# Rows that every partition needs: through a DRAM scratch and a read with partition step zero, in place of products with a selector

## The chip, the cores and the metric

One core of a Trainium2 chip runs the whole kernel. Times are device microseconds. The kernel before took 2334.57 us, the median of three runs (2333.76 to 2335.11).

## The reference, cut to what matters

Two layers of a backbone work on 256 context tokens and 256 latent tokens, 1024 features each, all in float32. Each layer is a half feed-forward step, three token mixers side by side (windowed attention, gated linear attention, mLSTM), and a second half feed-forward step. The last layer's output is wanted for the latent tokens only. The change is in the mLSTM, which has 4 heads of 128 and runs in both directions:

```python
def mlstm_scan(q, k, v, i_pre, log_f, carry):
    def step(carry, inp):
        C, n, m = carry
        b = jnp.cumsum(fc, axis=-1)
        log_w = jnp.where(tri, b[..., :, None] - b[..., None, :] + ic[..., None, :], -jnp.inf)
        log_inter = b + m[..., None]
        m_i = jnp.maximum(log_inter, jnp.max(log_w, axis=-1))
        w = jnp.exp(log_w - m_i[..., None])
        w_inter = jnp.exp(log_inter - m_i)
        s = jnp.einsum('bhid,bhjd->bhij', qc, kc) * w
        num = (w_inter[..., None] * jnp.einsum('bhid,bhde->bhie', qc, C)
               + jnp.einsum('bhij,bhje->bhie', s, vc))
        den = w_inter * jnp.einsum('bhid,bhd->bhi', qc, n) + jnp.sum(s, axis=-1)
        h = num / jnp.maximum(jnp.abs(den), jnp.exp(-m_i))[..., None]
        ...
```

For each direction and head there are numbers with one value per token: the gate sum in `log_w`, the factor `1 / max(|den|, exp(-m))` and that factor times `w_inter`. Each of them is multiplied or added to a matrix in which the token is the column, so it must be there on all 128 partitions.

## The kernel before, in words

Features lie on the 128 partitions and the 512 tokens (T) on the columns. Layer 0 works on all 512 columns; in layer 1 the query side of each mixer covers only the 256 latent columns (`cs = slice(c0, T)` with c0 = 256). A dense product splits float32 into two float32r parts and takes three matmuls (`acc<-xh,hi`, `acc<-xl,hi`, `acc<-xh,lo`) into an accumulator in PSUM of the pool `acc` (4 buffers); products of the mixers go into the PSUM pool `mx` (4 buffers). Weights come by SyncE's queue into `raw`; ACT writes the high part (L231) and DVE the low part (L232). Nearly every matmul has the line of the helper `mm`, L150; DVE's two-input operations have that of `tt`, L122, and ACT's functions that of `act`, L125.

The mLSTM runs per layer as one call of `mlstm_rows` and two calls of `mlstm`, one for each pair of heads. `mlstm_rows` makes the rows of all four heads and both directions in one tile: row 32 * q + hp belongs to direction and head parity q = 0 to 3 and to pair hp. A call of `mlstm` then builds states (L869) and weights within chunks, for which it needs the gate row `aa` on all partitions (`ab`, used in L883); sums the weights over the partitions with matmuls against `onec` or `onec2` ("the row sums"); makes den and its reciprocal (L905, L907) as rows; and needs both results on all partitions again (`rb`, `wb`) ahead of six matmuls for each of its two heads ("the outputs"), which the norm of the head follows (`head_norm`, with a column sum against `ones_h`, and L480, L481, L630 on DVE).

`bcast` (L833) makes such a tile: two matmuls into a `mx` buffer, whose stationary operand is one column of `sel`, repeated 128 times, so that the product picks row r; one for the high and one for the low part of the rows. The parts are made by `split`: a cast on ACT (L313) and a subtraction on DVE (L314).

The order on each engine is fixed ahead of the run by a scheduler of the tile framework: it takes the program's order as priority and moves work ahead when what it needs is there by its own estimates. So dense products of the mixer's later projections and output branches stand between the small matmuls of the mixers. The pools bound this: `W()` tiles (`t`) are 17, `F()` tiles (`f`) 25. POOL's queue holds, apart from additions for a norm (L493), only the reads that bring the residual back from a scratch in DRAM (`x<-xd`, L1130, 8 per layer).

After the mLSTM comes the attention (QK^T products into `mx` of 128x512, masks, L989 the maximum over keys, L990, exponentials, L999 the scaling, L1006 transposes, L1009 and L1011 copies, L1017), in layer 1 in four blocks.

Of the kernel before, what the change touches and what calls it, by code (L numbers as in the profile page):

```python
# [9 lines left out]
F32 = mybir.dt.float32  # L10
# [10 lines left out]
T = L + S  # L21
# [11 lines left out]
# columns of w_in, in the order the kernel consumes them (gate block first)  # L33
# [15 lines left out]
# columns of the small per-layer parameters  # L49
# [8 lines left out]
# shape-only float tables  # L58
# [19 lines left out]
def hybrid_backbone_kernel(ctx: ExitStack, tc: tile.TileContext, xT, cc, small, tables, lmask, crow, modw, modt,  # L78
# [42 lines left out]
    def tt(o, a, b, op):  # L121
        V.tensor_tensor(o, a, b, op)  # L122

    def act(o, i, f, **k):
        return A.activation(o, i, f, **k)  # L125
# [9 lines left out]
    def load(o, i):  # L135
        """a load; those of the start in the order of the program, and some later ones behind them."""
        d = nc.sync.dma_start(o, i)
        if loads and late[0] < 24:
            order(d, loads[-1])
        if starting[0]:  # L140
            loads.append(d)
        else:
            late[0] += 1

    def exp_ln_tables(after):
        """load the table set that serves both Exp and Ln, behind the activation `after`."""
        order(A.preload_act_table_set("natural_log_exp_and_others"), after, "table set of the next functions")  # L147

    def mm(o, l, r, start=True, stop=True):
        PE.matmul(o, l, r, start=start, stop=stop)  # L150

# [1 line left out]
    ct = res.tile([128, N_CT], F32, name="ct")  # L153
    sel = res.tile([128, 8], F32R, name="sel")
# [42 lines left out]
    def load_tables():  # L197
# [5 lines left out]
        V.tensor_copy(sel[:], C("selm"))  # L203

# [36 lines left out]
    def wunit_f(src, n, raw=None):  # L241
        """the same in tiles of the feature pool, for units that are wanted ahead of their turn."""
# [12 lines left out]
    def ahead(srcs):  # L255
        """the first two units of the next phase."""
# [12 lines left out]
    def dense_with(w, xs, cs):  # L269
        """one tile of 128 output features over the columns cs; K = 128 * len(xs)."""  # L270
# [8 lines left out]
    def dense_halves(ws, xs, done):  # L279
        """some tiles, one stream after the other: starts before the second stream is there."""  # L280
# [9 lines left out]
    def dense_tokens(src, xs):  # L290
        """512 output features with the tokens on partitions: one tile per chunk."""
# [33 lines left out]
    def start(src):  # L325
        """the first norm, the modulation it needs and the first products, as the weights come in."""
# [29 lines left out]
        def features(k):  # L356
            """modulation of the features 128 * k .., then these features of the norm."""
            with tc.high_priority() if k == 0 else ExitStack():
# [9 lines left out]
                for j in range(2):  # L368
                    mm(pt[:, 2 * j:2 * j + 2], sb[:, 128 * j:128 * j + 128], C("sel2"))
# [25 lines left out]
    def load_cond():  # L395
        """silu of the two conditioning vectors, on every partition."""
# [7 lines left out]
    def mod_vec(l, j, cond):  # L404
        """generator: modulation vector j of layer l on the vector engine, 128 features a step."""
# [46 lines left out]
    def mod_scale(l, j):  # L452
        """-0.5 * gain * (1 + scale) of norm j."""
# [7 lines left out]
    def mod_gate(l, j):  # L461
        """half of the gate of sub-layer j."""
# [10 lines left out]
    def neg2rstd(ms, cs, eps_col, eps):  # L473
        """-2 / sqrt(ms + eps): table value with one Newton step."""
# [11 lines left out]
    def square(k, c):  # L486
        """squares of one tile of the stream c, summed over the tiles but the last two."""
# [14 lines left out]
    def adaln(l, j, c0=0):  # L502
        """norm j of layer l: one call of the result for each stream, behind its last residual."""
# [50 lines left out]
    def turn(late, h, gate, nxt):  # L554
        """the last output tiles of a phase by streams, with the norm of the next phase behind each."""
# [11 lines left out]
    def ffn(l, j, c0, fill, pre, xn, side, nxt, head=None):  # L567
        """one half step; pre: the first weights, nxt: where those of the next phase are."""
# [44 lines left out]
    def log_sigmoid(z, bias, out_t, tmp):  # L613
        """log sigmoid(z + bias) = min(z + bias, 0) - ln(1 + exp(-|z + bias|))."""
# [6 lines left out]
    def head_norm(out, o, cs, gcol, eps_col, eps, tabled=True):  # L621
        """-2 * rmsnorm over the partitions of o (PSUM), times gcol."""
# [5 lines left out]
        mm(ms[:, cs], ones_h[:], sq[:, cs])  # L628
# [6 lines left out]
    def gla(l, ft, c0, gq, gk, gv, gb, gw2, gcol):  # L635
# [6 lines left out]
        for d in range(2):  # L642
            z = mx()
            mm(z[:], gw2[:, (2 * d + ft) * 128:(2 * d + ft + 1) * 128], gb[:])
# [13 lines left out]
        # states between chunks  # L658
# [3 lines left out]
        for d in range(2):  # L662
# [17 lines left out]
            for i, c in enumerate(ch):  # L680
                ps = mx()
                for hh in range(2):
                    mm(ps[64 * hh:64 * hh + 64, 0:128], kd[:, i * 128 + 64 * hh:i * 128 + 64 * hh + 64],
                       gv[c][:, hd(2 * ft + hh)])
# [7 lines left out]
        # within chunks  # L692
        att = []
        for hh in range(2):
            ps = mx()
            r = slice(64 * hh, 64 * hh + 64)
            for c in range(q0, 4):
                cc_ = slice(c * 128, (c + 1) * 128)
                mm(ps[:, cc_], gk[r, cc_], gq[r, cc_])
# [3 lines left out]
        for li, s in enumerate(LEVELS):  # L703
# [16 lines left out]
            for hh in range(2):  # L720
                ps = mx()
                r = slice(64 * hh, 64 * hh + 64)
                for c in range(q0, 4):
                    cc_ = slice(c * 128, (c + 1) * 128)
                    mm(ps[:, cc_], ek[r, cc_], eq[r, cc_])
# [4 lines left out]
        # outputs  # L730
# [28 lines left out]
    def conv_silu(l, ps, i, c0):  # L759
        """twice silu(conv(x) + b) of one tile of channels."""  # L760
# [18 lines left out]
    def mlstm_rows(l, gb):  # L779
        selgb = C("selgb")  # L780
        pi, pf = mx(), mx()
        mm(pi[:], selgb[:, 0:128], gb[:])
        mm(pf[:], selgb[:, 128:256], gb[:])
# [22 lines left out]
        # columns r = (head parity within direction q, head pair): index 2 * q + hp  # L806
# [18 lines left out]
        mm(ps[:, 0:64], ones_1[:], dd[:].rearrange("p a b -> p (a b)"))  # L825
# [511 lines left out]
```

## Time and profile before

| what | value |
|---|---|
| runs | 2333.76, 2334.57, 2335.11 us |
| profiled execution, span from first to last instruction | 2333.1 us |
| PE / DVE / ACT / POOL busy in it | 2291.4 / 1533.6 / 975.1 / 53.2 us |
| mean granted clock of TensorE | 0.996 of full speed |
| DMA, mean over the span | 135 GB/s |

The page gives the profiled execution no other time than its span, so the span stands for it below; it is 1.5 us under the median of the runs. PE is busy in nearly every slice of the span. Busy time of PE counts overlapping matmuls, so a mean duration of a group is longer than the spacing of its matmuls in a run.

### The profile page before, as it was taken

Reading aid. Unit: us, or ns where it says so; the run is one execution under the profiler, and the core shown is the slowest. Engines: PE = TensorE matmul, PEld = TensorE weight load, DVE = VectorE, ACT = ScalarE, POOL = GpSimd, SP = SyncE. Lnnn points to the kernel's source line nnn. Section 1 sums busy time; section 2 is a strip of 40 time slices with the busy share of each in tenths; the row PEclk is TensorE's granted clock in tenths of the full one; section 3 lists DMA queues with packets and bytes.
Section 4 is the critical chain, followed back from the end, with each engine's and each line's share of the span. In section 5 each row is a group of like instructions: output and inputs, shape, how many; then the busy total and the mean of one; then the engine's idle time right before and its main releaser. Section 6 shows DMA issues by size and latency. Waiting matters only on the chain. (4 is left out here: it accounts for less than half of the span.)

```text
span 2333.1 us, 32827 instructions
## 1 busy us (share of the span) xinstructions
PE 2291.4 (98%) x12496; PEld 1910.3 (82%) x12496; DVE 1533.6 (66%) x3213; ACT 975.1 (42%) x1569; POOL 53.2 (2%) x65
## 2 busy tenths in 40 slices
PE   7999999999999999999999999999999999999999
PEld 4888888777877667888888898888888788889999
DVE  4686875579865664658833357855545897877755
ACT  4322224445644542342222253222245665745443
POOL 0000001000000000100000000000010000001000
PEclk9999999999999999999999999999999999999999
DMA  7665554212211212436533236655433233335764
GB/s 282 210 200 159 187 187 129 91 48 66 82 55 64 64 46 81 147 111 198 173 113 99 76 115 208 202 160 188 157 114 103 88 100 100 109 120 183 241 199 145
DMA packets 117390, 314.94 MB, mean 135 GB/s; under 512 B 13296, under 2 KB 16240, under 8 KB 117104
## 3 DMA queue, kind: packets, MB, share of 16 engines
q1 hardware_dynamic: 116208, 309.69, 41.3%
q0 software_dynamic: 1024, 3.15, 0.4%
q8 instruction: 98, 1.61, 0.3%
q14 instruction: 60, 0.49, 0.1%
HBM read 308.59 MB, written 4.19 MB: 134 GB/s over the span
## 5 line engine op out<-in xcount | busy, mean ns | idle before, releaser
L231 ACT CAST hi<-raw 128x1024 fp32r<-128x1024 f32 (+2 forms) x446 | 434.6, 977 | 962.7 <-PE acc L150 637.4
L150 PE MATMUL acc<-xh,hi 128*128 128x512 f32 (+1 forms) x2192 | 784.5, 358 | 9.6 <-ACT xh L125 6.3
L150 PE MATMUL acc<-xl,hi 128*128 128x512 f32 (+1 forms) x2192 | 783.9, 358 | 0.2
L150 PE MATMUL acc<-xh,lo 128*128 128x512 f32 (+1 forms) x2192 | 781.7, 357 | 1.6 <-DVE lo L232 1.6
L232 DVE TENSOR_TENSOR lo<-raw,hi 128x1024 fp32r<-128x1024 f32 (+2 forms) x446 | 503.4, 1131 | 322.9 <-ACT hi L231 307.7
L150 PEld LDWEIGHTS acc<-xh,hi 128*128 128x128 f32 x2192 | 415.7, 190 | 76.8 <-ACT xh L125 8.7
L150 PEld LDWEIGHTS acc<-xl,hi 128*128 128x128 f32 x2192 | 415.7, 190 | 66.1 <-issue 8.8
L150 PEld LDWEIGHTS acc<-xh,lo 128*128 128x128 f32 x2192 | 415.7, 190 | 64.4 <-issue 6.7
L150 PE MATMUL acc<-f,hi 128*128 128x512 f32 (+1 forms) x1016 | 352.2, 347 | 0.0
L150 PE MATMUL acc<-f,lo 128*128 128x512 f32 (+1 forms) x896 | 314.1, 351 | 0.0
L415 DVE SCALAR_TENSOR_TENSOR u<-f,f 128x512 f32<-128x512 f32 x448 | 284.6, 685 | 12.7 <-DMA f<-in_modt_dram 12.7
L150 PE MATMUL acc<-t,hi 128*128 128x512 f32 (+1 forms) x824 | 287.1, 349 | 0.0
L150 PEld LDWEIGHTS acc<-f,hi 128*128 128x128 f32 x1016 | 192.2, 189 | 25.0 <-issue 1.2
L150 PEld LDWEIGHTS acc<-f,lo 128*128 128x128 f32 x896 | 169.7, 189 | 22.1 <-issue 0.4
L150 PEld LDWEIGHTS acc<-t,hi 128*128 128x128 f32 x824 | 155.8, 189 | 20.3
L122 DVE TENSOR_TENSOR t<-t,acc 128x512 f32<-128x512 f32 (+1 forms) x90 | 54.9, 610 | 154.8 <-PE acc L150 153.7
L539 DVE SCALAR_TENSOR_TENSOR x<-acc,ggt,x 128x256 f32<-128x256 f32 x136 | 61.1, 479 | 88.5 <-PE acc L150 88.4
L125 ACT ACTIVATE t<-t 128x512 f32<-128x512 f32 (+2 forms) x180 | 93.0, 529 | 58.3 <-DVE t L122 35.7
L122 DVE TENSOR_TENSOR t<-t,f 128x512 fp32r<-128x512 f32 (+3 forms) x172 | 99.2, 585 | 2.9 <-ACT f L313 2.1
L150 PE MATMUL mx<-t,t 64*128 64x128 f32 (+2 forms) x592 | 77.9, 288 | 0.9 <-DVE t L861 0.5
L150 PEld LDWEIGHTS mx<-t,t 64*128 64x128 f32 (+1 forms) x592 | 64.2, 188 | 16.3 <-issue 9.1
L150 PE MATMUL mx<-t,f 128*64 128x256 f32 (+3 forms) x352 | 69.8, 412 | 0.4
(209 smaller groups left out, 2167.3 us busy)
## 6 DMA issues: line engine op xcount, KB each, us to landing
raw<-in_w_dram SPq DMA_DIRECT2D x179, 512.0 KB, 3.6
f<-in_modt_dram SPq DMA_DIRECT2D x256, 256.0 KB, 4.5
raw<-in_win_dram SPq DMA_DIRECT2D x118, 512.0 KB, 3.5
raw<-in_w_dram SPq DMA_DIRECT2D x61, 384.0 KB, 3.1
raw<-in_w_dram SPq DMA_DIRECT2D x61, 320.0 KB, 3.0
raw<-in_wout_dram SPq DMA_DIRECT2D x24, 512.0 KB, 3.5
f<-in_modw_dram SPq DMA_DIRECT2D x32, 256.0 KB, 5.3
raw<-in_wo_dram SPq DMA_DIRECT2D x16, 512.0 KB, 3.8
```

The source lines that it names most:

```text
L122: V.tensor_tensor(o, a, b, op)
L125: return A.activation(o, i, f, **k)
L150: PE.matmul(o, l, r, start=start, stop=stop)
L231: a = A.copy(hi[:, :n], raw[:, :n])
L232: b = V.tensor_tensor(lo[:, :n], raw[:, :n], hi[:, :n].bitcast(F32), ALU.subtract)
L415: V.scalar_tensor_tensor(junk[:], raw[:], 1.0, cond[s][h][:], ALU.mult, ALU.mult, accum_out=part[:, k, s, h:h + 1])
L539: V.scalar_tensor_tensor(X[m][:, c], ps[:, c], gate[:, m, s:s + 1], X[m][:, c], ALU.mult, ALU.add)
```

## The change

`sel` and the split of the rows go. `rows_out` writes the rows of one tile into a scratch in DRAM with four DMAs of POOL's queue: for pair 0 two rows of each q, for pair 1 one row. The gate rows are written once per layer. `bcast` allocates a `W()` tile in SBUF and fills it with a DMA of POOL's queue, which reads one row of the scratch for each of the 128 partitions (partition step zero). Per layer there are 20 writes and 24 reads. The helpers `tt`, `act` and `mm` become other names of the engines' functions, so that matmuls and vector operations now have their own lines in a profile; comments go. The core of the diff:

```diff
@@ mlstm_rows
-        ah, al = F(F32R), F(F32R)
-        split(aa, slice(0, T), ah, al)
+        ad = rows_out(aa, 0, slice(0, T))
...
-        return dict(em=m, wi=wi, ah=ah, al=al, bc=bc, eb=eb, ws=ws)
-
-    def bcast(r, hi, lo, cs):
-        ps = mx()
-        s = sel[:, r:r + 1].to_broadcast([128, 128])
-        mm(ps[:, cs], s, hi[:, cs], True, False)
-        mm(ps[:, cs], s, lo[:, cs], False, True)
-        return ps
+        return dict(em=m, wi=wi, ad=ad, bc=bc, eb=eb, ws=ws)
+
+    def rows_out(t, hp, cs):
+        n = 2 if hp == 0 else 1
+        d = dp.tile([4, 2, T], F32, tag="rows", bufs=5, name=nm("rows"))
+        for q in range(4):
+            G.dma_start(d[q, hp:hp + n, cs], t[32 * q + hp:32 * q + hp + n, cs])
+        return d
+
+    def bcast(d, q, hp, cs):
+        t = W()
+        G.dma_start(t[:, cs], d[q, hp:hp + 1, cs].to_broadcast([128, cs.stop - cs.start]))
+        return t
@@ mlstm
-                ab = bcast(r, R["ah"], R["al"], cs)
+                ab = bcast(R["ad"], 2 * d + hl, hp, cs)
...
-        rh, rl, wh, wl = W(F32R), W(F32R), W(F32R), W(F32R)
-        split(nd, cs, rh, rl)
-        split(den, cs, wh, wl)
+        rd, wd = rows_out(nd, hp, cs), rows_out(den, hp, cs)
...
-                rb = bcast(r, rh, rl, cs)
+                rb = bcast(rd, 2 * d + hl, hp, cs)
...
-                wb = bcast(r, wh, wl, cs)
+                wb = bcast(wd, 2 * d + hl, hp, cs)
```

POOL's queue after the change, layer 1, second pair of heads (`rows` are the scratch buffers, `t` on the left of an arrow the tiles on 128 partitions; lines are those of the changed kernel):

```order
L828 DMA rows_16554<-t_16547 16x1x16 x4
L828 DMA rows_16559<-t_16546 16x1x16 x4
L834 DMA t_16564<-rows_16554 128x256
L834 DMA t_16567<-rows_16559 128x256
L834 DMA t_16571<-rows_16554 128x256
L834 DMA t_16574<-rows_16559 128x256
L834 DMA t_16600<-rows_16554 128x256
L834 DMA t_16603<-rows_16559 128x256
L834 DMA t_16607<-rows_16554 128x256
L834 DMA t_16610<-rows_16559 128x256
```

Eight writes and eight reads stand in one queue; the last four reads (head 1) take the slots of the first four, and wait until DVE has used these. Before, POOL had nothing in this place.

PE before, the same place, from the last dense product ahead of the selector products to the first of the second head (`mx_16615<-` and `_16636` are the first head's output and the second head's first row tile):

```order
L150 MATMUL acc_17092<-xh_14289,lo_17089 128x512
L150 MATMUL mx_16596<-t_16588,sel 128x256
L1117 MATMUL acc_17118<-ct,u_17085 128x128 x4
L150 MATMUL acc_17131<-xh_14275,hi_17127 128x512
...
L150 MATMUL mx_16609<-t_16591,sel 128x256
L150 MATMUL acc_17131<-xh_14275,lo_17128 128x512
...
L150 MATMUL mx_16615<-t_16491,f_15727 128x128
...
L150 MATMUL acc_17131<-xh_14281,hi_17127 128x512
...
L150 MATMUL mx_16626<-t_16623,ones_h 128x256
L150 MATMUL mx_16636<-t_16588,sel 128x256
```

And PE after the change, from the last of the 48 dense products behind the last row sum:

```order
L258 MATMUL acc_17799<-xh_14268,lo_17796 128x256
L927 MATMUL mx_16579<-t_16460,f_15707 128x128
L927 MATMUL mx_16579<-t_16569,t_16420 128x128
...
L619 MATMUL mx_16590<-t_16587,ones_h 128x256
L927 MATMUL mx_16615<-t_16520,f_15707 128x128
L927 MATMUL mx_16615<-t_16605,t_16480 128x128
...
L619 MATMUL mx_16625<-t_16623,ones_h 128x256
L937 MATMUL mx_17121<-t_17117,ct 128x512
L256 MATMUL acc_17832<-xh_14254,hi_17828 128x256
```

The dense products that stood between the two heads are ahead of the first head's outputs now; between `ones_h` of the first head and the outputs of the second there is none. On DVE (after the change) the norm of the first head (L471, L472, L621) comes ahead of the second head's products with its row tiles (L912, L915):

```order
L915 TENSOR_TENSOR t_16576<-f_15824,t_16574 128x256
L471 SCALAR_TENSOR_TENSOR t_16595<-mx_16590,t_16595 128x256
L472 SCALAR_TENSOR_TENSOR t_16595<-t_16595,t_16592 128x256
L621 SCALAR_TENSOR_TENSOR x_16586<-mx_16579,cols_14507,t_16595 128x256
L1080 SCALAR_TENSOR_TENSOR x_16586<-f_16136,x_16586 128x256
L912 TENSOR_TENSOR t_16520<-t_16520,t_16600 128x256
L915 TENSOR_TENSOR t_16605<-f_15865,t_16603 128x256
```

PE after the change in layer 1's attention, third of the four blocks, from its QK^T products (L979) to its transposes (L1000):

```order
L979 MATMUL mx_17554<-t_17343,f_17300 128x512
L979 MATMUL mx_17561<-t_17343,f_17300 128x512
L258 MATMUL acc_18350<-f_17327,lo_18299 128x256
L256 MATMUL acc_18387<-f_18365,hi_18383 128x256
L256 MATMUL acc_18406<-f_18365,hi_18383 128x256
L256 MATMUL acc_18431<-f_18365,hi_18427 128x256
L256 MATMUL acc_18450<-f_18365,hi_18427 128x256
L1000 MATMUL mx_17577<-ct,t_17545 128x128
```

Five dense products stand there; before the change there are 80 in this block (58 of them ahead of its first transpose) and 71 in the fourth, where now 20 stand.

## Rows read from the trace of the kernel before

**Rows 1.** The page, busy time of each engine (share of the span), instructions.

```profile
PE 2291.4 (98%) x12496; PEld 1910.3 (82%) x12496; DVE 1533.6 (66%) x3213; ACT 975.1 (42%) x1569; POOL 53.2 (2%) x65
```

**Rows 2.** Selector's tile: operations (ns min/median/max), then PE's idle time before them by releaser.

```profile
L150 PE MATMUL mx<-t,sel x64: 276/388/799, 658.0 to 1983.4; 128*128 128x512 f32 x32, 128*128 128x256 f32 x32
...
L150 PE MATMUL mx<-f,sel x32: 276/375/482, 633.3 to 1964.3; 128*128 128x512 f32 x16, 128*128 128x256 f32 x16
...
  ACT t L313: 3.5, 4
  DVE t L122: 1.1, 4
```

**Rows 3.** Timeline of PE: start, us, engine, line, operation, operands, shapes, count.

```profile
660.77 0.39 PE L150 MATMUL acc<-xh,hi 128*128 128x512 f32 x1
661.00 1.32 PE L150 MATMUL mx<-t,sel 128*128 128x512 f32 x5
...
2021.13 0.28 PE L150 MATMUL acc<-xh,lo 128*128 128x256 f32 x1
2021.25 0.28 PE L150 MATMUL acc<-xh,hi 128*128 128x256 f32 x1
```

**Rows 4.** Line L1130, POOL's DMA issues: ns min/median/max, first and last start.

```profile
L1130 POOL DMA_DIRECT2D x<-xd x16: 536/536/683, 944.3 to 2106.8; - x16
```

**Rows 5.** DMA issues: queue, count, KB each, median us from issue to landing.

```profile
f<-in_crow_dram SPq DMA_DIRECT2D x16, 256.0 KB, 6.3
...
x<-xd POOLq DMA_DIRECT2D x8, 256.0 KB, 4.3
...
xd<-x SPq DMA_DIRECT2D x8, 128.0 KB, 1.7
x<-xd POOLq DMA_DIRECT2D x8, 128.0 KB, 3.7
```

**Rows 6.** Tile in_crow_dram, SyncE's reads of one row to all partitions.

```profile
DMA to landing us min/median/max: 4.3/6.3/8.1
```

**Rows 7.** Timeline of PE, layer 1, second pair: row sum, then outputs.

```profile
1970.01 0.62 PE L150 MATMUL mx<-t,onec 128*32 128x256 f32 x2
...
1978.70 0.38 PE L150 MATMUL mx<-t,f 128*128 128x128 f32 x2
...
1979.59 0.61 PE L150 MATMUL mx<-t,t 128*128 128x128 f32 x4
```

**Rows 8.** Timeline of DVE there: factor times w_inter, end of head 0's norm.

```profile
1973.83 0.42 DVE L122 TENSOR_TENSOR t<-t,f 128x256 f32<-128x256 f32 x1
...
1984.75 0.48 DVE L630 SCALAR_TENSOR_TENSOR x<-mx,cols,t 128x256 f32<-128x256 f32 x1
```

**Rows 9.** Timeline of DVE, layer 0, second pair: den's sum and last product.

```profile
710.28 0.69 DVE L122 TENSOR_TENSOR t<-t,mx 128x512 f32<-128x512 f32 x1 [3.37 <-PE mx L150]
...
718.49 0.68 DVE L122 TENSOR_TENSOR t<-t,f 128x512 f32<-128x512 f32 x1
```

**Rows 10.** Timeline of DVE, layer 1's attention: mask, last maximum, scalings, next mask.

```profile
2051.80 0.30 DVE L122 TENSOR_TENSOR mx<-mx,ct 128x128 f32<-128x128 f32 x1 [0.56 <-PE mx L150]
...
2055.85 0.16 DVE L122 TENSOR_TENSOR e<-sm,mx 128x4 f32<-128x4 f32 x1
...
2061.89 1.27 DVE L999 TENSOR_SCALAR t<-t,l 128x512 f32<-128x512 f32 x3
...
2068.89 0.30 DVE L122 TENSOR_TENSOR mx<-mx,ct 128x128 f32<-128x128 f32 x1 [0.56 <-PE mx L150]
```

**Rows 11.** Timeline of ACT there: the block's last exponential.

```profile
2056.60 0.69 ACT L125 ACTIVATE t<-mx,mx 128x512 f32<-128x512 f32 x1
```

**Rows 12.** Windows: length; PE, PEld, DVE, ACT, POOL busy (count); PEclk, DMA share, GB/s.

```profile
2130.00:2134.00 4.00, 0.97 (x4) 0.30 (x2) 0.81 (x2) 2.97 (x5) 0.00 (x0) 0.91 0.00 0
2134.00:2138.00 4.00, 2.77 (x12) 2.62 (x13) 3.89 (x11) 2.26 (x6) 0.00 (x0) 0.50 0.00 0
2138.00:2142.00 4.00, 4.00 (x27) 4.00 (x27) 3.36 (x8) 2.93 (x5) 0.00 (x0) 0.74 0.00 0
```

**Rows 13.** The same view, the stretch of three of POOL's reads in layer 0.

```profile
944.00:948.00 4.00, 4.00 (x18) 3.10 (x18) 3.95 (x6) 1.06 (x1) 1.76 (x3) 1.00 0.79 253
```

More of the change, by code (lines that the diff above doesn't have):

```diff
@@ L119, in mx @@
         return pmx.tile([128, T], F32, tag="mx", name=nm("mx"))
[L121 to L125, printed above, removed]
+    tt, act, mm = V.tensor_tensor, A.activation, PE.matmul
     no_sync = mybir.DependencyInfo(mybir.DependencyClass.NoSync, mybir.DependencyReason.DATA)
@@ L147, in exp_ln_tables @@
         order(A.preload_act_table_set("natural_log_exp_and_others"), after, "table set of the next functions")
-    def mm(o, l, r, start=True, stop=True):
-        PE.matmul(o, l, r, start=start, stop=stop)
     ct = res.tile([128, N_CT], F32, name="ct")
-    sel = res.tile([128, 8], F32R, name="sel")
     lm = res.tile([128, len(LEVELS), 128], U8, name="lm")
@@ L627, in head_norm @@
         ms = mx()
-        mm(ms[:, cs], ones_h[:], sq[:, cs])
+        mm(ms[:, cs], ones_h[:], sq[:, cs], True, True)
         z = neg2rstd(ms, cs, eps_col, eps)
@@ L643, in gla @@
             z = mx()
-            mm(z[:], gw2[:, (2 * d + ft) * 128:(2 * d + ft + 1) * 128], gb[:])
+            mm(z[:], gw2[:, (2 * d + ft) * 128:(2 * d + ft + 1) * 128], gb[:], True, True)
             t1, t2, pr = W(), W(), W()
@@ L698, in gla @@
                 cc_ = slice(c * 128, (c + 1) * 128)
-                mm(ps[:, cc_], gk[r, cc_], gq[r, cc_])
+                mm(ps[:, cc_], gk[r, cc_], gq[r, cc_], True, True)
             a = W()
@@ L781, in mlstm_rows @@
         pi, pf = mx(), mx()
-        mm(pi[:], selgb[:, 0:128], gb[:])
-        mm(pf[:], selgb[:, 128:256], gb[:])
+        mm(pi[:], selgb[:, 0:128], gb[:], True, True)
+        mm(pf[:], selgb[:, 128:256], gb[:], True, True)
         ic, tmp, lf, b, m = W(), W(), W(), W(), F()
@@ L897, in mlstm @@
                         i = before[d][c]
-                        mm(qn[rr, cc_], Cs[d, hl][:, i * 160 + 128 - hp:i * 160 + 160 - hp], mq[heads[hl]][:, cc_])
+                        mm(qn[rr, cc_], Cs[d, hl][:, i * 160 + 128 - hp:i * 160 + 160 - hp], mq[heads[hl]][:, cc_], True, True)
                     else:
-                        mm(qn[rr, cc_], zero32[:], mq[heads[hl]][:, cc_])
+                        mm(qn[rr, cc_], zero32[:], mq[heads[hl]][:, cc_], True, True)
         den, nd = W(), W()
@@ L942, in qk_norm @@
         ms = mx()
-        mm(ms[:, cs], C("blk"), sq[:, cs])
+        mm(ms[:, cs], C("blk"), sq[:, cs], True, True)
         z = neg2rstd(ms, cs, 0, EPS)
@@ L950, in rope @@
         ps = mx()
-        mm(ps[:, ls], C("perm"), x[:, ls])
+        mm(ps[:, ls], C("perm"), x[:, ls], True, True)
         t = W()
@@ L961, in attention @@
             ps = mx()
-            mm(ps[:], C("dup", kv), kh[:])
+            mm(ps[:], C("dup", kv), kh[:], True, True)
             t = W()
@@ L984, in attention @@
                     ps = mx()
-                    mm(ps[:, 0:nk], aq[h // 2][r, qc], kd[kv][r, 0:nk])
+                    mm(ps[:, 0:nk], aq[h // 2][r, qc], kd[kv][r, 0:nk], True, True)
                     if lat:
```

16 lines of the change are left out of this document (7 added, 9 removed).

## Prediction, made before the result was known

> **What bounds the kernel now.** I read the page's busy times first. TensorE (PE) is busy for 2291.4 of 2333.1 us, so 41.7 us of idle time are all that better hiding could still give back, while VectorE (DVE) at 66%, ScalarE (ACT) at 42% and GpSimd (POOL) at 2% have room [rows 1]. So each matmul taken off PE shortens the kernel by the time of its columns, and each new wait that PE cannot fill lengthens it. PE's work stands in a fixed order; the question is where it waits afterwards. I read the selector products next, then the transfers that take their place, then, place by place, the chain from the last row sum to a head's output, and last what the clock does after a pause.
>
> **What goes.** The selector products are 64 + 32 = 96 matmuls, half of 512 columns, half of 256 [rows 2]. Listed durations overlap, so the price is the spacing in a run. Five of 512 columns take 1.32 us, of which the last one's own 0.39 us (its neighbours' duration) is tail: (1.32 - 0.39) / 4 = 0.23 us each; products of 256 columns follow each other at 2021.25 - 2021.13 = 0.12 us [rows 3]. 48 x 0.23 + 48 x 0.12 = 16.8 us. PE also stood idle ahead of them for 3.5 us on ACT's casts and 1.1 us on DVE's subtractions [rows 2], and both go: 4.6 us. Sum: -21.4 us. The casts and subtractions themselves, ten per layer, run on ACT and DVE beside a busy PE; I price them at nothing. The renamed helpers change no instruction.
>
> **What comes.** Per layer, POOL issues 20 small writes and 24 reads that copy a row to 128 partitions. The trace has no such pair. POOL's issues take 0.536 us each, 0.683 at most [rows 4]. For the landing the nearest rows are POOL's own reads of a plain layout, 4.3 us for 256 KB and 3.7 us for 128 KB; SP's queue already reads one row to all partitions, in 6.3 us at the median for 256 KB, and a write of 128 KB lands in 1.7 us [rows 5]. I take 3.7 and 4.3 us, because issuer, queue and bytes are those of the nearest rows, and keep 8.1 us, the slowest of SP's [rows 6], as the other end. The reads of the gate rows are issued far ahead, or behind a pair of heads that has dense work after it; I price them at nothing.
>
> The new chain of a pair is: reciprocal, four writes, product, four writes, four reads, four products, output. Take layer 1's second pair, and count from PE's last row sum, which ends at 1970.01 + 0.62 = 1970.63 [rows 7]. The last DVE operation ahead of the rows starts at 1973.83 and takes 0.42, to 1974.25, and the reciprocals are ready before it [rows 8]. Eight issues of 0.536 us from 1973.8 end at 1978.1, four reads at 1980.2. The fifth write is out at 1976.5 and landed about 1978.2, so the reads wait for it 0.1 us at most. The last read, issued by 1980.2, lands 3.7 us after its issue began, 1983.4, or ended, 1983.9. With one or two products of 0.42 [rows 8] the outputs start at 1984.5. PE's order has 48 products of 256 columns in between, 48 x 0.12 = 5.8 us, so PE is dry from 1976.4: a pause of 8.1 us.
>
> The second head of this pair follows with no dense work between. Head 0's outputs take from 1978.70 to 1979.59 + 0.61, 1.5 us [rows 7], now up to about 1986.0. In DVE's new order the whole norm of head 0 stands ahead of head 1's products. Before, that norm ended at 1984.75 + 0.48 = 1985.23 [rows 8], 5.0 us behind the outputs' end at 1980.20. So DVE comes to head 1 at 1991.0 and, with four products of 0.42, PE at 1992.6: a pause of 6.6 us. Head 1's four reads wait for head 0's tiles, are issued by 1986.7 and land by 1990.4, under the norm. Together +14.7 us. Bounds: +9 if half of the norm goes beside, +22 with reads of 8.1 us.
>
> The other three pairs have more behind them. Layer 1's first pair: 137 dense products, 137 x 0.12 = 16.4 us, against a chain of 1984.5 - 1970.6 = 13.9 us: nothing. In layer 0 the DVE part takes from 710.28 to 718.49 + 0.68 = 719.17, 8.9 us [rows 9]; eight more issues end at 13.2, the last read lands near 17.3, and a product of 0.68 with a conversion or two between makes 18 to 20 us. PE has 99 x 0.23 = 22.8 us in the first pair and 87 x 0.23 = 20.0 us in the second. I take +1 us, up to 5 with the slowest reads.
>
> **What is late next.** The dense work that now covers these places is taken from layer 1's attention. Its last two blocks had 80 and 71 dense products of 256 columns under the softmax, 9.6 and 8.5 us; now there are 5 and 20, 0.6 and 2.4 us. Before, a block lasts from mask to mask 2068.89 - 2051.80 = 17.1 us, and the last scalings end at 2061.89 + 1.27 = 2063.16 [rows 10]. Without the conversions of dense weights in between, the last exponential (0.69 us [rows 11]) would follow the last maximum at 2055.85 at once, the small sums and their reciprocal would take some 0.8 us, the four scalings 1.7: 2059.1. The 5.7 us from there to the next mask stay, so a block without dense work takes 13.1 us. Two blocks shrink by 4.0 each and lose 9.0 + 6.1 = 15.1 us of dense work, which others must find time for: +7.1 us. Bounds +3 (transposes pack closer, too) and +10 (conversions still in the way).
>
> **The clock.** Where PE was busy for only 0.97 of 4 us, from 2130 to 2134, the granted clock was 0.50 (1.2 GHz) in the next stretch and 0.74 in the one after, and 2.77 and 4.00 us of PE work lost 1.4 + 1.0 = 2.4 us by it [rows 12]. Pauses of 8 and 7 us will do the same to head 0's short outputs and to the dense work behind head 1: +2.5 us, 0 to 6.
>
> **A rule that speaks against the change.** POOL issued three of its reads between 944 and 948, with DVE busy for 3.95 of these 4 us [rows 13], and none of its issues took longer than 0.683 us [rows 4]. The Trainium skill, SBUF — State Buffer, "Who interferes with whom", says that a DVE operation in a two-port mode keeps GpSimd from writing the descriptors of its own DMAs; the page gives about 620 ns alone and 3100 ns beside such an operation as an example. Worked out from the page's figures, an estimate, reads beside such operations would come some 2.5 us later. The trace bears it out for none of the 16 issues. A lateness of that kind is the second rival, whose price is from rows.
>
> **Sum.** -21.4 + 14.7 + 1 + 7.1 + 2.5 = +3.9 us on the profiled execution's 2333.1 us: 2337.0. The median of the runs is 1.5 us above that span, so 2338.5 us.
>
> **The rivals.**
> - PE is mostly fed, and it is faster. For it: there is dense work in plenty, and POOL's issues of a row may be shorter than those of a tile; at 0.1 us, the twelve issues of a chain take 5.2 us less. Against: in PE's order 48 and then no dense products stand against a chain of 14 us. With half of the pauses gone, -21.4 + 7 + 4 + 1 = -9, about 2325 us; with none left, 2313.
> - The reads come late, and it is clearly slower. The place is the wait for a head's first products; the price is the landing. At 8.1 instead of 3.7 us [rows 6] head 0 of layer 1's second pair comes 4.4 us later and head 1 about 3.5 us, layer 1's first pair waits 13.9 + 4.4 - 16.4 = 2 us, layer 0's second 2 us: +12, about 2350 us. It decides from a landing of about 5 us on. For it: the only one-row reads in the trace are the slower kind. Against: they are on another queue, behind other loads.
> - The waits take exactly what the products give, 2334.6 us: the same terms, within the forecast's own range.
>
> **How the numbers follow.** A difference under 0.2%, 4.7 us, can't be told from no change here. The forecast's case, 2338.5 with its own range 2331 to 2345, holds 0.55, the late reads 0.22, the fed PE 0.23. About a third of the first lies above 2339.2 and next to nothing below 2329.9. So slower 0.40, within 0.36, faster 0.24. The range 2324 to 2350 takes in half of the pauses and the late reads, and leaves out a PE without any pause and the sum of all upper bounds.
>
> **What would show it.** In the profile after, PE's idle time is above 55 us while it has 96 matmuls less; PE waits for DVE 5 to 11 us ahead of the output products of layer 1's second pair, and 4 to 8 us ahead of the head behind it; it waits twice for 3 to 6 us in layer 1's attention; the granted clock is near 0.5 behind these. The first chain is wrong if POOL's issues of rows take far from 0.5 us or reads land outside 3.5 to 5 us, the attention's term if its last blocks stay at 17 us, and the whole forecast if PE has no wait above 3 us at these places.

## The result, and the profile after

The changed kernel takes 2367.62 us, the median of four runs, against 2334.84 us for the kernel before in the same job: a ratio of 1.0140 (95% interval 1.0127 to 1.0154). It is slower by 33 us, where the forecast was slower by 4 with a range up to 2350. The sign was right, the size was far off.

The page of the changed kernel, busy time of each engine, answers to [rows 1]:

```profile
PE 2293.3 (97%) x12400; PEld 1908.6 (81%) x12400; DVE 1529.6 (65%) x3202; ACT 980.0 (41%) x1566; POOL 99.3 (4%) x153
```

PE has 96 matmuls less and is busy for 1.9 us more. Its idle time has grown from 41.7 to 2367.7 - 2293.3 = 74.4 us. So there are two things to find: 33 us of new idle time, and some 19 us by which the work that is left has become slower. Nearly all of the second is the clock, whose mean over the span went from 0.996 to 0.984: PE's busy time times (1 - granted clock), added up in windows of 2 us, went from 8.3 to 25.4 us.

Layer 0 did what was hoped. From its first write of the residual to POOL's first read of it back it took 944.3 - 346.4 = 597.9 us before and 936.6 - 348.2 = 588.4 us after, 9.5 us less. Layer 1, from its write of the residual to the end, took 2333.1 - 1743.1 = 590.0 us and takes 2367.7 - 1735.5 = 632.2 us: 42.2 us more. The table splits these by the same windows: idle time is what PE isn't busy, and clock loss is the product above.

| stretch of layer 1 | before: idle, clock loss | after: idle, clock loss | change |
|---|---|---|---|
| first pair of heads, from its last row sum to that of the second | 0.1, 0.0 | 5.4, 2.8 | +8.1 |
| second pair, from there to the attention's first mask | 1.4, 0.0 | 23.1, 7.1 | +28.8 |
| attention, to 18 us behind the last block's first mask | 4.1, 0.0 | 11.9, 5.2 | +13.0 |

The sum is +49.9; less the 5.8 us of selector products that layer 1 no longer has it is +44.1, against the 42.2 measured.

Windows of the changed kernel (columns as in [rows 12]): the first pair's pause; the second pair's; the last two blocks of the attention:

```profile
1936.00:1952.00 16.00, 12.64 (x80) 12.09 (x79) 5.47 (x9) 4.98 (x6) 3.74 (x7) 0.79 0.62 162
1996.00:2012.00 16.00, 4.71 (x27) 4.21 (x26) 4.76 (x9) 1.28 (x2) 8.14 (x16) 0.66 0.64 146
2012.00:2020.00 8.00, 2.80 (x9) 2.11 (x10) 3.52 (x9) 3.14 (x6) 0.00 (x0) 0.50 0.09 11
2020.00:2036.00 16.00, 10.25 (x43) 8.21 (x42) 5.23 (x11) 11.53 (x18) 0.00 (x0) 0.63 0.00 0
2101.00:2119.00 18.00, 11.60 (x51) 6.81 (x51) 10.55 (x30) 5.09 (x13) 0.00 (x0) 0.72 0.10 30
2119.00:2134.00 15.00, 10.40 (x60) 6.92 (x57) 8.41 (x26) 4.98 (x13) 1.06 (x2) 0.89 0.07 19
```

The first number behind the window's length is PE's busy time, the seventh its granted clock. From 2012 to 2020 PE does 2.8 us of work in 8, at 1.2 GHz.

The second pair in detail. POOL's queue in the changed kernel, which had nothing here before:

```profile
1996.30 3.86 POOL L828 DMA_DIRECT2D rows<-t  x8 [24.55 <-DVE t L904]
2000.15 0.56 POOL L834 DMA_DIRECT2D t<-rows  x1
2001.89 1.60 POOL L834 DMA_DIRECT2D t<-rows  x3 [1.19 <-DMA rows<-t]
2004.59 0.54 POOL L834 DMA_DIRECT2D t<-rows  x1 [1.10 <-DMA t<-rows]
```

Eight writes start behind the reciprocal (L904), the first read goes out, and the next waits 1.19 us until a write has landed. DVE there:

```profile
1992.67 1.22 DVE L223 TENSOR_TENSOR lo<-raw,hi 128x1024 fp32r<-128x1024 f32 x1
...
1994.25 1.75 DVE L904 RECIPROCAL t<-t 128x256 f32<-128x256 f32 x1
1995.94 1.23 DVE L223 TENSOR_TENSOR lo<-raw,hi 128x1024 fp32r<-128x1024 f32 x1
...
2003.87 0.43 DVE L912 TENSOR_TENSOR t<-t,t 128x256 f32<-128x256 f32 x1 [3.87 <-DMA t<-rows]
2006.26 0.43 DVE L915 TENSOR_TENSOR t<-f,t 128x256 f32<-128x256 f32 x1 [1.97 <-DMA t<-rows]
2007.86 0.43 DVE L912 TENSOR_TENSOR t<-t,t 128x256 f32<-128x256 f32 x1 [1.17 <-DMA t<-rows]
```

Two conversions of dense weights stand inside the chain, one ahead of the reciprocal and one behind it, and the products wait for the reads. PE waits for all of it:

```profile
2008.80 0.80 PE L927 MATMUL mx<-t,f 128*128 128x128 f32 x2 [11.02 <-DVE t L917]
2012.20 1.22 PE L619 MATMUL mx<-t,ones_h 128*128 128x256 f32 x2 [0.47 <-ACT t L615]
2018.42 0.77 PE L927 MATMUL mx<-t,f 128*128 128x128 f32 x2 [5.00 <-DVE t L917]
...
2024.47 1.46 PE L937 MATMUL mx<-t,ct 128*128 128x512 f32 x2 [1.98 <-ACT t L935]
2029.22 0.58 PE L256 MATMUL acc<-xh,hi 128*128 128x256 f32 x1 [3.30 <-ACT f L1086]
```

The last two rows are waits that the forecast didn't have: the attention's norm and the next dense product wait for ACT. From the end of the last row sum (1991.83) to head 0's outputs there are 17.0 us; it was 8.1 us before [rows 7]. In the first pair it is 20.0 us (1924.56 to 1944.54), before 10.2.

The transfers (issues with ns min/median/max; then us from issue to landing, min/median/max; reads first, writes second):

```profile
L834 POOL DMA_DIRECT2D t<-rows x48: 536/536/577, 584.3 to 2009.6; - x48
...
DMA to landing us min/median/max: 3.1/4.1/7.2
```

```profile
L828 POOL DMA_DIRECT2D rows<-t x40: 484/518/672, 445.5 to 1999.7; - x40
...
DMA to landing us min/median/max: 1.6/2.6/5.0
```

By size, the reads' medians are 4.3 us for 256 KB and 3.9 us for 128 KB, the writes' 2.0 us for 4 KB, 3.2 us for 2 KB and 2.6 us for 1 KB. The small writes take longer than the 1.7 us of the 128 KB write that I took them for. The medians of the reads are near what I took, but they hide what matters here, since they take in reads that go out alone. These are the four reads ahead of head 0 in the second pair:

```profile
L834 POOL DMA_DIRECT2D t<-rows x4: 536/541/555, 2000.1 to 2003.0; - x4
...
DMA to landing us min/median/max: 3.7/4.9/5.6
```

One by one they land 3.7, 4.3, 5.4 and 5.6 us after their issue, and 4.0, 4.5, 5.4 and 5.7 us in the first pair; layer 1's four reads of the gate rows ahead of these, which go out one at a time, take 3.1 to 3.6 us. DVE, which waits for them, is idle while the second pair's four are issued.

In the attention, the mask that begins the third block and the one that begins the fourth (DVE, changed kernel) answer to [rows 10]:

```profile
2101.92 0.30 DVE L982 TENSOR_TENSOR mx<-mx,ct 128x128 f32<-128x128 f32 x1 [0.55 <-PE mx L979]
...
2119.04 0.29 DVE L982 TENSOR_TENSOR mx<-mx,ct 128x128 f32<-128x128 f32 x1
```

17.1 us, as before, though 75 of its 80 dense products have gone. The lines between these two masks tell why:

```profile
2104.73 1.22 DVE L223 TENSOR_TENSOR lo<-raw,hi 128x1024 fp32r<-128x1024 f32 x1
...
2108.89 1.68 DVE L993 TENSOR_SCALAR t<-t,l 128x512 f32<-128x512 f32 x4
```

```profile
2106.59 0.38 PE L256 MATMUL acc<-f,hi 128*128 128x256 f32 x1 [3.18 <-DVE u L1099]
2109.52 1.57 PE L1000 MATMUL mx<-ct,t 128*128 128x128 f32 x4 [2.55 <-DVE t L993]
```

```profile
2107.00:2117.00 10.00, 6.80 (x28) 4.31 (x30) 4.10 (x12) 2.04 (x5) 0.00 (x0) 0.50 0.14 50
```

The last scalings end at 2108.89 + 1.68 = 2110.57, 8.7 us behind the mask, where it was 11.4 before [rows 10]: one conversion of weights is left on DVE in place of three, and none on ACT. From there to the next mask it takes 8.5 us, before 5.7. PE had waited for 3.18 and 2.55 us, and from 2107 to 2117 the granted clock is 0.50 (1.2 GHz), while from 2111.8 PE goes from product to product until the next mask's scores. So what the softmax gained, the slow clock took back.

### The profile page after: what moved, and what is told of

It is laid out like the page before. It is cut to its first block, busy times and chain, and to the rows that moved or that the text cites. A ratio compares the mean times of both kernels' runs of the same rounds, so it can differ in the third digit from the quotient of the medians.

```text
span 2367.7 us, 32797 instructions
## 1 busy us (share of the span) xinstructions
PE 2293.3 (97%) x12400; PEld 1908.6 (81%) x12400; DVE 1529.6 (65%) x3202; ACT 980.0 (41%) x1566; POOL 99.3 (4%) x153
## 5 line engine op out<-in xcount | busy, mean ns | idle before, releaser
L256 PE MATMUL acc<-xh,hi 128*128 128x512 f32 (+1 forms) x2192 | 785.3, 358 | 13.1 <-ACT xh L521 6.3
L256 PE MATMUL acc<-f,hi 128*128 128x512 f32 (+1 forms) x896 | 313.9, 351 | 4.2 <-DVE u L1099 3.2
L406 DVE SCALAR_TENSOR_TENSOR u<-f,f 128x512 f32<-128x512 f32 x448 | 284.7, 685 | 11.1 <-DMA f<-in_modt_dram 10.9
L257 PE MATMUL acc<-t,hi 128*128 128x512 f32 (+1 forms) x704 | 248.2, 353 | 0.0
L256 PEld LDWEIGHTS acc<-f,hi 128*128 128x128 f32 x896 | 169.5, 190 | 28.0 <-DVE u L1099 3.4
L257 PEld LDWEIGHTS acc<-t,hi 128*128 128x128 f32 x704 | 133.2, 189 | 18.2
L484 POOL TENSOR_TENSOR t<-t,t 128x256 f32<-128x256 f32 x45 | 44.4, 1003 | 1125.7 <-ACT t L480 1125.7
L257 PE MATMUL acc<-x,hi 128*128 128x512 f32 (+1 forms) x192 | 65.3, 342 | 0.1
L304 ACT CAST f<-t 128x512 fp32r<-128x512 f32 (+1 forms) x90 | 50.3, 559 | 23.7 <-DVE t L542 22.1
L471 DVE SCALAR_TENSOR_TENSOR t<-mx,t 128x256 f32<-128x256 f32 (+1 forms) x36 | 19.2, 533 | 58.7 <-ACT t L470 58.6
L305 DVE TENSOR_TENSOR t<-t,f 128x512 fp32r<-128x512 f32 (+1 forms) x90 | 54.7, 607 | 2.1 <-ACT f L304 2.1
```

The lines of the kernel that those rows point to most:

```text
L256: mm(o, wh, xh[:, cs], start=first, stop=False)
L257: mm(o, wh, xl[:, cs], start=False, stop=False)
L304: A.copy(hi[:, cs], src[:, cs])
L305: tt(lo[:, cs], src[:, cs], hi[:, cs].bitcast(F32), ALU.subtract)
L406: V.scalar_tensor_tensor(junk[:], raw[:], 1.0, cond[s][h][:], ALU.mult, ALU.mult, accum_out=part[:, k, s, h:h + 1])
L471: V.scalar_tensor_tensor(u[:, cs], ms[:, cs], eps, u[:, cs], ALU.add, ALU.mult)
```

## The experiments

"Before" in each is the kernel before on the same chip in the same job. Theory 1 in all of them: the loss is the scratch's round trip, exposed where PE's order has too little dense work.

**Layer 0 alone.** Layer 1 keeps the selector products.

```diff
+AB = ('dma', 'sel')                          # gate rows, by layer
+RW = (('dma', 'dma'), ('sel', 'sel'))        # factors, by layer and pair
```

> Layer 0 as in the changed kernel, layer 1 with the selector products of before. Theory 1 (the loss is the wait for the scratch's round trip in layer 1, where PE has too little dense work in its order): the layer-0 part gains, about 9 us, so about 2326 us (2322 to 2330). Theory 2 (the transfers themselves disturb the kernel wherever they run): no gain, 2333 us or more.

2326.74 us, ratio 0.9965 (0.9954 to 0.9977). As theory 1 had it: where the dense work covers the round trip, the transfers gain most of what layer 0's products cost (48 x 0.23 = 11.0 us by the forecast's spacing). All of the loss is layer 1's.

**Gate rows alone**, `AB = ('dma', 'dma')`, factors by selector products.

> Only the gate rows go through the scratch (8 of the 24 reads of a layer), the factors of the denominators by selector products. Theory 1: these reads lie far ahead of their use, so their third of the selector products, 5.6 us, is gained in both layers: about 2329 us (2325 to 2333). A rival, that the 8 buffers which the reads take from the pool of t tiles reorder the dense work and cost as much: 2335 us or more.

2335.99 us, ratio 1.0010 (1.0001 to 1.0020): the time that the rival gave. No engine waits for these reads in layer 1, yet it shows two new pauses of PE, 2.65 us for DVE and 3.49 us for ACT, that eat the gain. A changed order has a price of its own; that it comes from the eight buffers is not shown.

**Reads that need no fresh row.** The reads of the factors take the gate rows' scratch.

```diff
-                rb = bcast(rd, 2 * d + hl, hp, cs)
+                rb = bcast(R["ad"], 2 * d + hl, hp, cs)
```

> All writes and reads stay, but the reads of the denominators' factors take the gate rows' scratch, so that they wait for no reciprocal and no write (the output is not the reference's). Theory 1: with the wait gone the whole gain shows, 2335 - 16.8, about 2318 us (2312 to 2328). Theory 2 (traffic, POOL's issues or the row reads themselves cost the time): it stays near 2365 us, above 2350.

2354.93 us, ratio 1.0094 (1.0073 to 1.0114): not theory 1, and above the 2350 us of theory 2, though 10 us short of its 2365. My test was weak, since the reads still stood behind the eight writes in POOL's one queue, and these wait for the reciprocal. Only the wait for the landing was gone; the chains became 16.3 and 13.4 us.

**Without the writes as well**, so that nothing in POOL's queue waits for a reciprocal.

```diff
-        rd, wd = rows_out(nd, hp, cs), rows_out(den, hp, cs)
```

> No rows of the denominators are written, and the 16 reads of a layer that carried them take the gate rows' scratch instead (the output is not the reference's). POOL's queue then has no write that waits for a reciprocal. Theory 1 (the wait for the round trip costs the time): the gain of 16.8 us shows, about 2318 to 2330 us. Rival (the reads hang on the 17 buffers of the pool of t tiles, which come free late whatever the data): 2345 us or more, with POOL waiting for DVE ahead of its reads.

2346.62 us, ratio 1.0055 (1.0040 to 1.0070): theory 1 alone can't be all. POOL did wait for DVE ahead of its reads, 12.8 and 13.2 us in layer 1's two pairs, for free `t` buffers. So that went next.

**The same with 21 buffers for `t`** (and 21 for `f`, so that it fits).

> As the run without rows of the denominators (reads of the gate rows' scratch in their place; the output is not the reference's), and with 21 buffers for t tiles and 21 for f tiles. If that run's 11 us over before came from late buffers, they go here: about 2336 us (2330 to 2341). If the dense work is pulled ahead of the attention all the same (its last blocks have 21 and 20 dense products in the order, before 80 and 71), the attention's loss remains: 2343 us or more.

2342.40 us, ratio 1.0040 (1.0026 to 1.0054). The time lies between the two expectations, but this run is the most telling one. No row is waited for and the two chains are short, 10.1 and 11.8 us, near those of before. Windows of this run: the stretch of the second pair's chain, then the last two attention blocks:

```profile
1970.00:1982.00 12.00, 12.00 (x99) 11.87 (x99) 10.69 (x17) 4.55 (x7) 1.06 (x2) 1.00 0.57 179
2072.00:2089.00 17.00, 12.62 (x61) 8.03 (x59) 10.77 (x28) 6.32 (x14) 0.00 (x0) 0.70 0.20 63
2089.00:2107.00 18.00, 13.34 (x85) 9.85 (x83) 10.77 (x32) 6.36 (x16) 2.14 (x4) 0.91 0.10 30
```

PE never pauses in the first row; the order has put 97 dense products there, as if a transfer had to be waited for. The attention still loses 10.5 us of idle time and 5.5 of clock. So this loss comes from the order alone, from dense work that it pulls ahead, whether or not a wait is there.

**One pair at a time in layer 1.** First pair: `RW = (('dma', 'dma'), ('dma', 'sel'))`; second pair: `('sel', 'dma')`; gate rows of layer 1 by selector products in both.

> Layer 0 as changed; layer 1's first pair of heads takes the denominators' factors through the scratch, the second pair and all gate rows by selector products. Theory 1: layer 0 gives 8 us, the first pair loses about what its own pauses show in the changed kernel, 7 us, less 2 us of selector products: about 2332 us (2328 to 2337). If every dense product that is used up early is missing under the attention at full price: 2340 us or more.

> Layer 0 as changed; in layer 1 only the second pair of heads takes its factors through the scratch, the first pair and the gate rows by selector products. The order has 87 dense products ahead of head 0 and 71 between the heads; the attention's last two blocks have 5 and 20 dense products as in the changed kernel. If the attention's loss comes from dense work used up ahead, it is there in full (12 us with the clock), and the pair's own pauses are small: about 2341 us (2336 to 2347). If the pair's own round trip is the loss: 2334 us with an undisturbed attention.

2344.59 us, ratio 1.0034 (1.0019 to 1.0048), and 2342.75 us, ratio 1.0023 (1.0013 to 1.0033). The first is what was expected if dense work that is used up early is missing in the attention, and so is the second. By the ratios, the first pair alone costs 16 us and the second alone 14 us over the run of layer 0 alone, and in both the attention has its full loss (10.4 idle and 5.9 clock; 11.9 and 5.2). All of layer 1's rows together cost 41 us. That is more than 16 and 14, although the attention's loss of some 13 us is in each of these and only once in the 41. What grows is the second pair's own idle time: 5.5 us alone, 23.1 us in the changed kernel, where the order has left it 48 dense products ahead of head 0 and none between the heads, in place of 87 and 71. Part of the difference can be the gate rows, which go through the scratch only in the changed kernel; this isn't separated.

**Dense work held back.** The dense products of the last two gates in layer 1, and so all behind them, are put behind the second attention block.

```diff
+        if first and hold[0] is not None:
+            order(i, hold[0])
+            hold[0] = None
```

> The changed kernel, where the dense products of the last two gates in layer 1, and all behind them, are held behind the second attention block's products of queries and keys. PE's order through the mLSTM is as it was; dense work goes from the stretch ahead of the attention and its first blocks into its last blocks (60 and 72 products there) and behind it. If the dense work is a fixed sum that covers one wait or another, what the attention gains is lost ahead of it: 2362 to 2372 us. If only the distribution was bad: 2358 us or less.

2375.97 us, ratio 1.0167 (1.0147 to 1.0187), slower than either expectation. Windows: ahead of the attention, its first stretch, its last two blocks:

```profile
2034.00:2050.00 16.00, 5.19 (x26) 3.90 (x25) 6.37 (x11) 15.72 (x25) 0.00 (x0) 0.74 0.20 66
2058.00:2072.00 14.00, 7.65 (x30) 4.18 (x28) 8.48 (x27) 4.16 (x11) 0.00 (x0) 0.65 0.00 0
2088.00:2104.00 16.00, 15.48 (x114) 11.65 (x114) 11.51 (x29) 8.26 (x18) 0.00 (x0) 1.00 0.28 90
2104.00:2121.00 17.00, 16.09 (x126) 13.59 (x124) 13.79 (x32) 8.08 (x18) 0.00 (x0) 1.00 0.31 95
```

The last two blocks are whole again (PE idle for 0.5 and 0.9 us, clock 1.00), and the time is lost ahead of them, with interest: part of the dense work now lies behind the attention, where it covers nothing. Dense work covers one wait or another, not both.

**Fewer transfers.** One write of four rows in place of four, and in layer 1 one read for two tiles.

```diff
+        G.dma_start(d[:, hp, cs], t[hp:128:32, cs])
```

> The four writes of a row tile become one, and in layer 1 the two reads of a head become one: 2 writes and 2 reads ahead of a first head in place of 8 and 4. Theory 1: 8 issues of 0.53 us go from the chain in layer 1, and the order then has 96 dense products ahead of head 0 of the second pair and 62 between its heads in place of 48 and none; the pauses there fall from 18 us to about 5, and with them the clock's loss: about 2343 us (2334 to 2352). A rival, that the price is the latency of write and read alone, not the number of issues: above 2357 us.

2362.87 us, ratio 1.0125 (1.0109 to 1.0140): the rival's time, and not clearly another than the changed kernel's. The chains are 21.8 and 15.5 us, no shorter on the whole. POOL waits 3.27 us for the write's landing ahead of the first pair's first read, and the reads of two tiles land far later than the single ones of layer 1, which took 3.1 to 5.7 us:

```profile
L845 POOL DMA_DIRECT2D t<-rows x8: 711/726/766, 1934.9 to 1995.1; - x8
...
DMA to landing us min/median/max: 6.6/8.1/10.3
```

So what fewer issues gave, later landings took. What the issues alone cost, this run doesn't tell.

**Outputs of both heads ahead of both norms.**

```diff
-            head_norm(outs[-1], o, cs, gcol, 0, EPS, hl == 0)
+        for hl, o in enumerate(os):
+            outs.append(O())
+            head_norm(outs[-1], o, cs, gcol, 0, EPS, hl == 0)
```

> Both heads' outputs come ahead of both norms in the program. The order then has 122 dense products ahead of head 0 of layer 1's second pair and 20 between the heads, in place of 48 and none. Theory 1: head 0's pause falls from 11.0 to about 2 us, head 1's to 2 us, the attention has less dense work left: about 2352 us (2345 to 2360). If the dense work is only moved from one pause to the next (what is not under the scratch is missing under the attention): 2362 us or more.

2355.88 us, ratio 1.0093 (1.0078 to 1.0108), within the expected span. The second pair's idle time falls from 23.1 to 14.8 us; the attention is as empty as before (10.9 and 5.8).

**More buffers alone**, 21 `t` and 21 `f`, all else as changed.

> 21 buffers for t tiles in place of 17, 21 for f tiles in place of 25. If the reads hang on free t buffers, they are issued earlier, the order has 128 dense products ahead of head 0 of layer 1's second pair and 49 between its heads, the pauses there fall by about 13 us and some clock is kept: about 2350 us. If the dense work used there is missing in the attention in any case and the round trip alone counts: 2358 us or more.

2360.75 us, ratio 1.0101 (1.0086 to 1.0116): the second pair gains 11 us of idle time, the first loses 5. Buffers are a part of the loss, 9 us of 33 by the ratios, while the rows are waited for.

**The clock.** 14 matmuls on ready data in the second pair's pause, and then 22 and 9 in both of its pauses.

```diff
+            for i in range(14):
+                mm(warm[:, cs], ones_h[:], den[:, cs], True, True)
```

> The changed kernel with 14 more matmuls of 256 columns on data that is ready, between the 48 dense products and head 0's outputs in layer 1's second pair; all else in PE's order is as it was. They take about 6.6 us of the 11 us that PE waits there. If the granted clock after the pause is a part of the price, it stays at 1.00 longer and the kernel is 2 to 5 us faster, about 2364 us (2361 to 2367). If the pause's length alone counts, it is 2368 us, as before, or some more.

> The changed kernel with 22 more matmuls of 256 columns on ready data ahead of head 0's outputs in layer 1's second pair, and 9 more behind its norm's column sum; the rest of PE's order is as it was. They fill the pauses of 11.0 and 5.0 us almost wholly. If the granted clock is a part of the price (6.9 us of the loss in this stretch by the rows of the changed kernel), the kernel gains 3 to 6 us: about 2363 us. If only the pauses' length counts: 2368 us or somewhat more.

2366.58 us, ratio 1.0136 (1.0121 to 1.0152), and 2366.64 us, ratio 1.0125 (1.0110 to 1.0141). Neither can be told from the changed kernel's 1.0140. In the second, the pauses fell to 1.85 and 2.37 us, head 0's outputs ran at full clock, and the two ACT waits behind head 1 stayed at 1.98 and 3.30 us. But the filling kept only 3 us of clock: the stretch's clock loss is about 4 us there, 7.1 in the changed kernel. In the one profiled execution of each, the way from the second pair's last row sum to the attention's first mask takes 73.4 us in place of 75.2. A gain of that size is inside the intervals. So how much of the 15 us of clock loss in layer 1 is on the path stays open for the pauses; in the attention's third block it is on it.

**The queue.** All rows by ACT's queue, and by SyncE's.

```diff
-            G.dma_start(d[q, hp:hp + n, cs], t[32 * q + hp:32 * q + hp + n, cs])
+            nc.sync.dma_start(d[q, hp:hp + n, cs], t[32 * q + hp:32 * q + hp + n, cs])
```

> All writes and reads of rows are issued by ACT in place of POOL. If the issuing queue is the price (POOL's 0.53 us an issue, or descriptors that it writes late beside DVE), the chain from the last row sum to head 0 gets 3 us or more shorter in layer 1 and the kernel 5 to 10 us faster: about 2360 us. If the landing and the used-up dense work are the price: 2365 us or more, and ACT's own casts for the weights stand behind its waiting issues.

> All writes and reads of rows are issued by SyncE, whose writes of the residual took 0.33 us to issue and 1.7 us to land, in the queue of the weight loads. If the issuing queue is the price: the chain gets 3 us or more shorter, the order has 111 dense products ahead of head 0 of layer 1's second pair: about 2357 us (2350 to 2362). If not, 2365 us or more; weight loads that stand behind waiting rows would make it slower still.

ACT: 2371.51 us, ratio 1.0160 (1.0145 to 1.0175). SyncE: 2356.99 us, ratio 1.0096 (1.0081 to 1.0111). SyncE issues a write in 0.251 us in place of 0.518:

```profile
L828 SPq DMA_DIRECT2D rows<-t x40: 214/251/309, 443.7 to 1985.7; - x40
```

With it the first pair's chain is 16.2 us in place of 20.0 and its pause nearly gone (0.32 us); the second pair's is 19.1 in place of 17.0, and the attention is as empty as ever (11.7 and 6.0). ACT issues in 0.263 us, but its chains are 22.0 and 16.2. The Trainium skill, DMA: Bandwidth & Descriptors, "SWDGE vs HWDGE vs iDMA", says that SP and ACT generate descriptors in hardware with a faster setup than GpSimd's software. The issue times agree. But the two hardware queues differ by 14.5 us here, and the kernel with ACT's is no faster than that with POOL's, so the time of an issue doesn't decide by itself. The other work in the queue may, weight loads on SyncE's and casts on ACT's; that isn't shown, since PE's order changed with the queue, too.

**Layer 0 alone, by SyncE's queue.**

> Rows through the scratch in layer 0 alone, as in the run that gained 7 us, with the transfers issued by SyncE in place of POOL. Layer 0's dense work already covers the round trip, so the queue should not matter there: about 2326 us (2323 to 2329). If the weight loads queued behind the waiting rows are late in layer 0: 2331 us or more.

2323.14 us, ratio 0.9949 (0.9936 to 0.9963): faster than both kernels, and the best version found. Its interval overlaps that of layer 0 alone by POOL, so the queue's part isn't shown.

## Why the prediction was wrong, step by step

- The products, -16.8 us: near. Layer 0's share is 48 x 0.23 = 11.0, less the 1 us forecast for its waits; layer 0 gave 9.5 us, and layer 0 alone 7 to 8 us in the runs.
- The idle time ahead of them, -4.6 us: misread. [rows 2] adds up the idle time of the weight loads (PEld), which run beside the matmuls, and that of PE. PE itself waited for a split only once, for 1.26 us, so 3.3 us of the gain were never there:

```profile
1974.84 0.38 PE L150 MATMUL mx<-t,sel 128*128 128x256 f32 x1 [1.26 <-ACT t L313]
```

- POOL's issues, 0.536 us: right. The reads' landing, 3.7 and 4.3 us: right for the medians (3.9 and 4.3), too short where it counts, with 5.4 to 5.7 us for the last two of a chain's four reads in layer 1. The writes' landing, 1.7 us: too short (medians 2.0 to 3.2).
- The chain of 13.9 us: too short, 17.0 and 20.0. Of the 3.1 us in the second pair, 1.0 is DVE's conversion ahead of the reciprocal (its end, 1994.25 + 1.75 = 1996.00, less 1991.83 is 4.2 us, forecast 3.2), 1.2 POOL's wait for the landed write, and most of the rest the reads' landing. The first pair has two conversions ahead of its reciprocal, which makes 2.1 us, and POOL waits 1.95 us for a write. In the forecast I took DVE's order of before, which had no conversion in between.
- "Layer 1's first pair: 137 dense products ... nothing" failed by that: 16.4 us of cover, 20.0 us of chain.
- Head 0's pause, 8.1 us, was 11.0; head 1's, 6.6 us, was 5.0. The mechanism and the place were right. What I did not look for is what follows: two more waits, 1.98 and 3.30 us, for ACT. Its last norm and a table load of 1.28 us stand ahead of the tanh (L1086) that empties the accumulator which the next dense product needs.
- The attention, +7.1 us: the step that failed is "so a block without dense work takes 13.1 us". The third block took 17.1. Of the 4.0 us, 1.4 are in its softmax, where one conversion of 1.22 us was left (8.7 us, forecast 7.3). The larger part, 2.8 us, is in "The 5.7 us from there to the next mask stay": they became 8.5, at a granted clock of 0.50 from 2107 to 2117. The loss was +13.0.
- The clock, +2.5 us: 15.1 us of loss is counted in these stretches of layer 1. In the attention some of it is on the path; filling the second pair's pauses gave nothing that could be measured.
- The rule that spoke against the change: no lateness of that kind shows. The 48 reads were issued in 0.536 to 0.577 us each, and in the second pair DVE was idle while the four reads went out that then landed late. The rival built on late reads had the better time (2350), and it is right in part: the median landing of 4.1 us is under the 5 us from which it was to decide, but the reads that head 0 waits for pass it. What they add is 1 to 2 us a pair, not the 4.4 that it priced.

The forecast's frame held: products off PE against waits on PE, with dense work taken from the attention. It broke in the sizes. The terms for layer 1's waits, 14.7 + 7.1 + 2.5 = 24.3 us, measured 49.9: chains longer by 3 and 6 us, waits for ACT behind them, and blocks of the attention that did not get shorter. With the 3.3 us of idle time that was never there, this is nearly the whole of the miss. Two of the prediction's own signs of being wrong are there: reads that land outside 3.5 to 5 us in the chains, and an attention block that stays at 17 us. The dense work of layer 1 is one stock; the order took 126 products from the attention's last two blocks, which costs 12 to 13 us there even where, as in the run with 21 buffers and without writes, no row is waited for.

## What to carry to other kernels

When a change turns a short wait into a long one, ask where the work that will cover it stood before, and price that place too, at the clock that PE is granted there once it waits: count the independent work of the stage as a stock and the chains as claims on it. In layer 0, with enough in stock, the same edit gains; so decide such an exchange stage by stage. Take a chain's length from the new order on every engine it passes, conversions and drains of others included; take the landing of a small write from small writes, and that of a read from the last of as many as go out in a row. A list of waits by tile can mix engines: check on the engine's own lines that it was the bottleneck that waited.

## What was not expected of the hardware

- A write of 2 KB to DRAM landed in 3.2 us at the median and one of 4 KB in 2.0, both slower than 1.7 us for 128 KB by SyncE. The place in the row tells more than the size: of the second pair's eight writes of 1 KB the first two landed 1.6 us after their issue and the third 3.7 us.
- Four reads issued in a row landed later one by one, 3.7 to 5.6 us after their issue, and reads of two tiles 6.6 to 10.3 us. Why isn't shown.
- One write of four rows in place of four writes did not shorten the first pair's way to its first read: POOL waited 3.27 us for its landing.
- Keeping PE busy in the pauses with 31 more matmuls neither cost nor gained anything that could be measured.
